# Norm phase of a gated attention/mLSTM layer: the second low part ahead of the modulation sum in two tiles, and wider dummy products

## The chip, the cores and the metric

One core of a Trainium2 chip runs the whole kernel in one launch. The metric is device time in microseconds (us); lower is better. The time before is a median over 3 executions; one further execution was profiled.

The engines are named as in the profile: PE (TensorE, matrix products) with PEld (its weight loads), DVE (VectorE), ACT (ScalarE), POOL (GpSimd) and SP (SyncE, which here issues the DMAs). Each engine works through its own instructions in the order in which the program lists them, and waits only where an operand or a buffer isn't ready.

## The reference, cut to what matters

One layer: a conditioning vector `c` modulates an RMS norm, the result goes through one large projection, then attention and a chunked mLSTM, gates and an output projection. Only the first lines bear on the change:

```
ada = c @ w_ada + b_ada                       # [1, 3*1024]
shift, scale, gate = split(ada, 3)
h = rmsnorm(x, norm_w) * (1 + scale) + shift  # [256, 1024]
... = split(h @ w_in, ...)                    # w_in is [1024, 11272]
```

All is float32, with 256 tokens and a width of 1024.

## The kernel before

**Precision.** A product of two float32 matrices is made of three products of rounded parts: each operand is split into a high part (a cast to the one-pass type fp32r) and a low part (the operand minus its high part), and high·high, high·low and low·high are summed. The high part of a weight tile is a cast on ACT, the low part a subtraction on DVE.

**Norm phase (lines 105 to 311).** The 1024 input features are eight row tiles k = 0..7 of 128. The phase computes the normed and modulated `h` transposed, tile by tile, and at once multiplies each tile with the first 1792 columns of `w_in`, summing over k in four PSUM banks (`pm`, the last one called `pg`). For tile k the DMAs bring `adat[k]`, two halves of [128, 1024] of `w_ada` (s = 1 for scale, s = 0 for shift; four buffers), and `wrow[k]`, the rows of `w_in` in two pieces. The order of all work is written out by hand in the string `P1_STEPS` (lines 42 to 45): one letter for an operation, one digit for a tile or a count. The letters that matter, in their order for a tile k from 1 to 6:

- `b` (L160, ACT): turns the shift sum into a bias column. `i`, `j` (L166, L170, ACT): modulate the tile into `hTh` (high part) and `hf` (full).
- `U` (L183, DVE): low part of `w_in` columns 0 to 511. `G` (L173, DVE): `hTl`, the low part of `h`, from `hf`.
- `x` (L178, ACT): high part of columns 512 to 1023. `L`: SP issues the next two loads.
- `c` of tile k+1 (L152, DVE): the scale sum, a product of `adat[k+1]` with the broadcast `c`, summed along the row. It needs half s = 1 of `adat[k+1]`.
- `z` (L183, DVE): low part of columns 512 to 1023 of tile k. It needs `x`.
- `y` (L178, ACT): high part of columns 1024 to 1791. `a`, `w` of tile k+1 (L156, L178, ACT): scale column from the sum, and the next tile's first high part.
- `k` of tile k+1 (L152, DVE): the shift sum. `v` (L183, DVE): low part of columns 1024 to 1791 of tile k.
- `e` (L194, PE): the tile's 24 products. Bank 0 takes three pairs (with `hTh`·high, `hTh`·low, `hTl`·high), bank 1 three pairs, of which the third uses the low part from `z`, then banks 2 and 3 with high parts, and last the two pairs that use the low part from `v`.

So DVE runs through `U G c z k v` for each tile, and `U` of the next tile follows `v`.

**The beginning.** `keep_clock(n)` (lines 223 to 225) multiplies the identity by itself n times into a PSUM tile that nobody reads. It is called with WARM = 5 ahead of the four products `pc` that spread `c` over the partitions (L233), and again by the step `K5` right behind them. ACT copies `pc` to `cb` (L236), squares the second half of `x` (L239), and makes `diag`, the identity scaled by the reciprocal norm (L242, two halves of tokens, with POOL in between at L213 and L214). Then PE transposes and scales `x` with `diag` as the moving operand (steps D and E, L255), ACT modulates tile 0 out of PSUM (L166), and the products of tile 0 start (step P, L194). DVE computes tile 0's sums at L145, which read `cb`.

**Behind the norm phase** PE goes through the other columns of `w_in` and the three projections (lines 957 to 997), with ACT and DVE splitting each weight tile (L440, L444) a few tiles ahead.

Of the kernel before, what the change touches and what calls it, by code (L numbers as in the profile page):

```python
# [38 lines left out]

P1_STEPS = ("K5 D0 D1 D2 E0 E1 E2 C0 w0 R0 R1 R2 R3 U0 H0 G0 t0 B0 P0 x0 z0 y0 t2 B1 t1 L1 c1 a1 w1 k1 v0 Q0 q0 n0 T3 m0 "
            + "".join(f"b{k} i{k} U{k} j{k} G{k} x{k} " + ("t3 " if k == 2 else "") + f"L2 c{k + 1} z{k} y{k} a{k + 1} "
                      f"w{k + 1} k{k + 1} v{k} e{k} " for k in range(1, 7))
            + "b7 i7 U7 j7 G7 x7 z7 y7 v7 P7 Q7 q7 N7 M7").split()
WARM = 5

KX = 248
NR = 1536 + KX + 8
# [15 lines left out]
def tile_hybrid(ctx: ExitStack, tc: tile.TileContext, x, c, params, params2, w_row, ada_mod, ada_gate,  # L65
                w_in, w_att_proj, w_ml_proj, w_out, out):
    nc = tc.nc
# [15 lines left out]
    ident = consts.tile([128, 128], F32, name="ident")  # L83
# [65 lines left out]
    def modulation_sum(k, s):  # L149
        if s:  # L150
            sums[k] = ph.tile([128, 2], F32, name="sums", bufs=2)
        nc.vector.tensor_tensor_reduce(sq, adat[k][:, s], cb, 1.0, 0.0, OP.mult, OP.add, sums[k][:, s:s + 1])  # L152
# [9 lines left out]
    def modulate(k, parts="ij"):  # L162
        kc = slice(k, k + 1)
        src = xnT[:, k] if k else xps[0][:, 0]
        if "i" in parts:
            nc.scalar.activation(hTh[:, k], src, AF.Identity, scale=Ab[:, kc], bias=Bb[:, kc])  # L166
        if "j" not in parts:
            return
        hf[k] = ph.tile([128, S], F32, name="hf", bufs=2)
        nc.scalar.activation(hf[k], src, AF.Identity, scale=Ab[:, kc], bias=Bb[:, kc])  # L170
# [4 lines left out]
    def split_hi(k, c0, c1, copy=nc.scalar.copy):  # L175
        if k not in wsp:
            wsp[k] = (ph.tile([128, NR], F32R, name="wrh", bufs=3), ph.tile([128, NR], F32R, name="wrl", bufs=3))
        copy(wsp[k][0][:, c0:c1], wrow[k][:, c0:c1])  # L178

    def split_low(k, e, c0, c1):  # L180
        h, l = wsp[k]
        cs = slice(c0, c1)
        e.tensor_tensor(l[:, cs], wrow[k][:, cs], h[:, cs].bitcast(F32), op=OP.subtract)  # L183
# [37 lines left out]
    pw = pp.tile([128, 2, 512], F32, name="warm", tag="pm0")  # L221

    def keep_clock(n):
        for _ in range(n):
            nc.tensor.matmul(pw[:, 0, 0:128], ident, ident, start=True, stop=True)

    keep_clock(WARM)


    pc = [pp.tile([128, 512], F32, name="pc0", tag="pg"), pp.tile([128, D], F32, name="pc1", tag="pm2")]  # L230
    for j in range(4):
        n, q = divmod(j, 2)
        nc.tensor.matmul(pc[n][:, q * 256:(q + 1) * 256], pick[:, j:j + 1].to_broadcast([128, 128]), cparts,  # L233
                         start=q == 0, stop=q == 1, skip_group_check=True)
# [35 lines left out]
    def some(*what):  # L270
        return lambda k: [mm_row(k, ch, (i,)) for ch, i in what]
# [22 lines left out]

    for step in P1_STEPS:
        op, k = step[0], int(step[1])
        if op == "L":
            next_loads(k)
        else:
            dict(C=modulation, H=modulate, R=rel_prep, K=keep_clock, T=x_transposes, t=x_copy, B=open_banks,  # L300
                 D=lambda k: x_transposes(k, (0,)), E=lambda k: x_transposes(k, (1,)),
                 w=lambda k: split_hi(k, 0, 512), x=lambda k: split_hi(k, 512, 1024), y=lambda k: split_hi(k, 1024, NR),
                 U=lambda k: split_low(k, nc.vector, 0, 512), z=lambda k: split_low(k, nc.vector, 512, 1024),
                 v=lambda k: split_low(k, nc.vector, 1024, NR), G=modulate_low,
                 c=lambda k: modulation_sum(k, 1), k=lambda k: modulation_sum(k, 0),
                 a=modulation_scale, b=modulation_shift, i=lambda k: modulate(k, "i"), j=lambda k: modulate(k, "j"),
                 P=lambda k: mm_row(k, 0), Q=lambda k: mm_row(k, 1, (0, 1)), q=lambda k: mm_row(k, 1, (2,)),
                 N=lambda k: mm_row(k, 2), M=lambda k: mm_row(k, 3),
                 n=some((2, 0), (2, 1), (3, 0), (3, 1)), m=some((2, 2), (3, 2)),
                 e=some((0, 0), (0, 1), (0, 2), (1, 0), (1, 1), (1, 2), (2, 0), (2, 1), (3, 0), (3, 1), (2, 2), (3, 2))  # L310
                 )[op](k)
# [187 lines left out]
    f = slice(32, 36)  # L499
# [424 lines left out]
    for g in range(NG):  # L924
# [32 lines left out]
        for kk in range(2):  # L957
            k = 2 * kp + kk
            first, last = k == 0, k == KT - 1
            if ch["name"] == "out":  # L960

                for i in (0, 1):
                    for t, c0 in ((0, 0), (0, 256), (1, 0), (1, 256)):
                        a = (sh_, sl_)[i][:, k, t * 128:(t + 1) * 128]
                        cs = slice(c0, c0 + 256)
                        for w in (wh, wl)[:2 - i]:
                            nc.tensor.matmul(mmt[ci][:, t, cs], a, w[:, kk, cs],  # L967
                                             start=first and i == 0 and c0 == 0 and w is wh,
                                             stop=last and i == 1 and c0 > 0, skip_group_check=True)
            elif ch["kind"] == "tok":  # L970
                for t in range(2):
                    a, b = sh_[:, k, t * 128:(t + 1) * 128], sl_[:, k, t * 128:(t + 1) * 128]
# [14 lines left out]
    for t, c0, n in ((0, 0, 512), (1, 0, 256), (1, 256, 256)):  # L987
        pt = ps.tile([128, n], F32, name="mm", bufs=2)
        for k in range(KT):
            a, b = T["yh"][:, k, t * 128:(t + 1) * 128], T["yl"][:, k, t * 128:(t + 1) * 128]  # L990
# [54 lines left out]
```

## Time and profile before

| | |
|---|---|
| median of 3 runs | 353.72 us (353.4 to 353.92) |
| profiled execution, its own time | 354.01 us |
| its span in the profile | 352.2 us |
| PE busy | 345.3 us (98%) |
| DVE / ACT / POOL busy | 240.7 / 209.9 / 83.0 us |

A row of a timeline gives the start in us from the span's start, the time in us, the engine, the line of the kernel, the operation with output and inputs, how many instructions are merged, and in brackets how long the engine was idle before and what ended that. A row that merges n instructions ends with the end of the last one. Matmuls are pipelined: each is listed with its whole duration though the next starts earlier, so the pace of a row is its time less one duration, over n - 1.

### The profile page before, as it was taken

To read this page: it belongs to the slowest core of one execution; us is meant where nothing else is said; L and a number is where in the kernel's file an instruction comes from. 1 tells how busy PE (TensorE), PEld (TensorE's weight loads), DVE (VectorE), ACT (ScalarE), POOL (GpSimd) and SP (SyncE) were. 2 spreads that over 40 slices of the span, in tenths; PEclk is the share of its full clock that TensorE was granted. 3 is DMA by queue.
4 is the path that set the end of the run, shared out by engine and by line. 5 is a ranking of instruction groups with operands and counts; after the bars stand their busy time and mean duration, and the time that the engine had idled before them with its cause. 6 is when DMAs were issued, how large, how long until landed. Compare 5 with 4: busy or idle time off the path is not lost.

```text
span 352.2 us, 6126 instructions
## 1 busy us (share of the span) xinstructions
PE 345.3 (98%) x2424; PEld 321.0 (91%) x2424; DVE 240.7 (68%) x363; ACT 209.9 (60%) x328; POOL 83.0 (24%) x79
## 2 busy tenths in 40 slices
PE   7999999999999999999999999999999999999996
PEld 6778889888999999999999888888899999999995
DVE  5889988869974428767774474764475775469961
ACT  4867789996885766674654435545646374544510
POOL 4700006582006052555240000000010320452000
PEclk9999999999999999999999999999999999999999
DMA  8999999995680453493664955649219229382011
GB/s 299 418 417 419 412 384 337 237 261 217 220 308 13 139 220 125 147 370 137 239 241 131 378 207 214 265 151 379 66 26 359 95 60 358 123 271 88 2 61 60
DMA packets 25140, 77.98 MB, mean 221 GB/s; under 512 B 2960, under 2 KB 6040, under 8 KB 24600
## 3 DMA queue, kind: packets, MB, share of 16 engines
q1 hardware_dynamic: 24816, 77.03, 61.3%
q10 hardware_dynamic: 296, 0.56, 0.5%
q8 instruction: 19, 0.31, 0.4%
q14 instruction: 9, 0.07, 0.1%
HBM read 76.14 MB, written 1.45 MB: 220 GB/s over the span
## 4 chain that ended last, share of the span: by engine, by line
PE 92%; DMA 7%; DVE 0%; issue 0%; DVEq 0%
PE mm L984 15%; PE mm L981 15%; PE mm L983 15%; PE mm L974 9%; PE mm L975 9%; PE mm L976 9%; PE pm L194 6%; DMA adat<-in_ada_mod_dram 6%; PE mm L967 3%; PE aux L737 1%; PE pg L194 1%; PE mm L996 1%; PE aux L634 1%; PE mm L995 1%; PE mm L994 1%; DMA xt<-in_x_dram 1%
## 5 line engine op out<-in xcount | busy, mean ns | idle before, releaser
L444 DVE TENSOR_TENSOR wl<-raw,wh 128x1024 fp32r<-128x1024 f32 (+1 forms) x92 | 115.8, 1268 | 68.0 <-ACT wh L440 68.0
L440 ACT CAST wh<-raw 128x1024 fp32r<-128x1024 f32 (+1 forms) x100 | 102.2, 1031 | 58.8 <-PE mm L976 29.4
L981 PE MATMUL mm<-hTh,wh 128*128 128x256 f32 x320 | 90.1, 282 | 0.0
L983 PE MATMUL mm<-hTl,wh 128*128 128x256 f32 x320 | 88.7, 277 | 0.0
L984 PE MATMUL mm<-hTh,wl 128*128 128x256 f32 x320 | 88.7, 277 | 0.0
L981 PEld LDWEIGHTS mm<-hTh,wh 128*128 128x128 f32 x320 | 60.2, 188 | 0.1
L983 PEld LDWEIGHTS mm<-hTl,wh 128*128 128x128 f32 x320 | 60.2, 188 | 0.1
L984 PEld LDWEIGHTS mm<-hTh,wl 128*128 128x128 f32 x320 | 60.2, 188 | 0.0
L974 PE MATMUL mm<-wh,hTh 128*128 128x512 f32 (+1 forms) x144 | 55.0, 382 | 0.0
L976 PE MATMUL mm<-wh,hTl 128*128 128x512 f32 (+1 forms) x144 | 54.4, 378 | 0.0
L975 PE MATMUL mm<-wl,hTh 128*128 128x512 f32 (+1 forms) x144 | 54.3, 377 | 0.0
L976 PEld LDWEIGHTS mm<-wh,hTl 128*128 128x128 f32 x144 | 27.0, 188 | 5.1
L974 PEld LDWEIGHTS mm<-wh,hTh 128*128 128x128 f32 x144 | 27.0, 188 | 4.7
L975 PEld LDWEIGHTS mm<-wl,hTh 128*128 128x128 f32 x144 | 27.1, 188 | 4.6
L444 POOL TENSOR_TENSOR wl<-raw,wh 128x1024 fp32r<-128x1024 f32 x8 | 19.5, 2456 | 18.4 <-ACT wh L440 18.4
L774 POOL TENSOR_SCALAR f<-f 128x4 f32<-128x4 f32 x2 | 0.4, 198 | 86.9 <-DVE f L773 86.9
L183 DVE TENSOR_TENSOR wrl<-raw,wrh 128x512 fp32r<-128x512 f32 (+1 forms) x24 | 18.1, 781 | 0.5 <-ACT wrh L178 0.4
L981 PE MATMUL mm<-yah,wh 128*128 128x256 f32 x64 | 18.3, 286 | 0.0
L152 DVE CUSTOM_DVE_ANT_0 sq<-adat,cb 128x1024 f32<-128x1024 f32 x14 | 17.1, 1221 | 1.1 <-DMA adat<-in_ada_mod_dram 1.1
L984 PE MATMUL mm<-yah,wl 128*128 128x256 f32 x64 | 17.7, 277 | 0.0
L983 PE MATMUL mm<-yal,wh 128*128 128x256 f32 x64 | 17.7, 277 | 0.0
L981 PE MATMUL mm<-ymh,wh 128*128 128x256 f32 x64 | 17.7, 276 | 0.0
(218 smaller groups left out, 663.8 us busy)
## 6 DMA issues: line engine op xcount, KB each, us to landing
raw<-in_w_in_dram SPq DMA_DIRECT2D x36, 1024.0 KB, 4.9
adat<-in_ada_mod_dram SPq DMA_DIRECT2D x16, 512.0 KB, 9.3
raw<-in_w_row_dram SPq DMA_DIRECT2D x8, 640.0 KB, 9.4
raw<-in_ada_gate_dram SPq DMA_DIRECT2D x4, 1024.0 KB, 5.6
raw<-in_w_att_proj_dram SPq DMA_DIRECT2D x4, 1024.0 KB, 7.9
raw<-in_w_ml_proj_dram SPq DMA_DIRECT2D x4, 1024.0 KB, 5.5
raw<-in_w_out_dram SPq DMA_DIRECT2D x4, 1024.0 KB, 4.8
raw<-in_w_row_dram SPq DMA_DIRECT2D x8, 256.0 KB, 9.3
```

The source lines that it names most:

```text
L152: nc.vector.tensor_tensor_reduce(sq, adat[k][:, s], cb, 1.0, 0.0, OP.mult, OP.add, sums[k][:, s:s + 1])
L183: e.tensor_tensor(l[:, cs], wrow[k][:, cs], h[:, cs].bitcast(F32), op=OP.subtract)
L194: nc.tensor.matmul(pm[ch][:, t], a[:, k, t * 128:(t + 1) * 128], b[:, cs], start=k == 0 and i == 0 and (ch < 3 or t == 0), stop=k == KT - ...
L440: nc.scalar.copy(h, w)
L444: e.tensor_tensor(l, w, h.bitcast(F32), op=OP.subtract)
L967: nc.tensor.matmul(mmt[ci][:, t, cs], a, w[:, kk, cs], start=first and i == 0 and c0 == 0 and w is wh, stop=last and i == 1 and c0 > 0, sk ...
L974: nc.tensor.matmul(o, a, wh[:, kk], start=first, stop=False)
L975: nc.tensor.matmul(o, a, wl[:, kk], start=False, stop=False)
L976: nc.tensor.matmul(o, b, wh[:, kk], start=False, stop=last)
L981: nc.tensor.matmul(o, wh[:, kk, cs], sh_[:, k], start=first and i % 2 == 0, stop=False, skip_group_check=True)
L983: nc.tensor.matmul(o, wh[:, kk, cs], sl_[:, k], start=False, stop=False, skip_group_check=True)
L984: nc.tensor.matmul(o, wl[:, kk, cs], sh_[:, k], start=False, stop=last and i % 2 == 1, skip_group_check=True)
```

## The change

In tiles 2 and 3 the order of `c` and `z` is swapped, so that DVE makes the second low part of tile k ahead of the scale sum of tile k+1. In the other tiles the order stays. The dummy products at the beginning are 3 instead of 5, in both places, and each has 512 moving columns (the identity four times over) instead of 128.

```diff
-P1_STEPS = ("K5 D0 D1 D2 E0 E1 E2 C0 w0 R0 R1 R2 R3 U0 H0 G0 t0 B0 P0 x0 z0 y0 t2 B1 t1 L1 c1 a1 w1 k1 v0 Q0 q0 n0 T3 m0 "
-            + "".join(f"b{k} i{k} U{k} j{k} G{k} x{k} " + ("t3 " if k == 2 else "") + f"L2 c{k + 1} z{k} y{k} a{k + 1} "
-                      f"w{k + 1} k{k + 1} v{k} e{k} " for k in range(1, 7))
+P1_STEPS = ("K3 D0 D1 D2 E0 E1 E2 C0 w0 R0 R1 R2 R3 U0 H0 G0 t0 B0 P0 x0 z0 y0 t2 B1 t1 L1 c1 a1 w1 k1 v0 Q0 q0 n0 T3 m0 "
+            + "".join(f"b{k} i{k} U{k} j{k} G{k} x{k} " + ("t3 " if k == 2 else "") + f"L2 "
+                      + (f"z{k} c{k + 1} " if k in (2, 3) else f"c{k + 1} z{k} ") + f"y{k} a{k + 1} w{k + 1} k{k + 1} v{k} e{k} " for k in range(1, 7))
             + "b7 i7 U7 j7 G7 x7 z7 y7 v7 P7 Q7 q7 N7 M7").split()
-WARM = 5
+WARM = 3
...
     def keep_clock(n):
         for _ in range(n):
-            nc.tensor.matmul(pw[:, 0, 0:128], ident, ident, start=True, stop=True)
+            nc.tensor.matmul(pw[:, 0].rearrange("p (r n) -> p r n", r=4), ident, ident[:, None, :].to_broadcast([128, 4, 128]),
+                             start=True, stop=True)
```

## The prediction

> **What bounds the kernel now.** I read the page first, for the bound, then PE's own waits, then the timelines of DVE, ACT and PE around the places that the change touches.
>
> ```profile
> span 352.2 us, 6126 instructions
> ...
> PEclk9999999999999999999999999999999999999999
> ...
> PE 92%; DMA 7%; DVE 0%; issue 0%; DVEq 0%
> PE warm L225 <- POOL ident masks.py:199: 1.4, 1, 1.4
> PE xps L255 <- ACT diag L242: 0.8, 1, 0.8
> PE pm L194 <- DVE wrl L183: 0.6, 1, 0.6
> PE pm L194 <- ACT hTh L166: 0.5, 1, 0.5
> ```
>
> The chain that ended last is PE for 92% of the span, and the last four rows are all the waits of PE that the profile lists. The next rows place them: before 25 us. Behind that PE never waits, so whatever the norm phase gains or loses reaches the end one to one, unless a new wait is made. The profiled execution took 354.01 us, 1.8 more than its span; that is 0.3 above the median of the runs, 353.72. I add my sum to both.
>
> ```profile
> 21.31 0.43 DVE L173 TENSOR_TENSOR hTl<-hf,hTh 128x256 fp32r<-128x256 f32 x1
> 22.85 1.22 DVE L152 CUSTOM_DVE_ANT_0 sq<-adat,cb 128x1024 f32<-128x1024 f32 x1 [1.11 <-DMA adat<-in_ada_mod_dram]
> 24.00 0.69 DVE L183 TENSOR_TENSOR wrl<-raw,wrh 128x512 fp32r<-128x512 f32 x1
> 24.60 1.22 DVE L152 CUSTOM_DVE_ANT_0 sq<-adat,cb 128x1024 f32<-128x1024 f32 x1
> 25.75 1.55 DVE L183 TENSOR_TENSOR wrl<-raw,wrh 128x768 fp32r<-128x768 f32 x2
> 27.66 1.22 DVE L152 CUSTOM_DVE_ANT_0 sq<-adat,cb 128x1024 f32<-128x1024 f32 x1
> 29.41 1.22 DVE L152 CUSTOM_DVE_ANT_0 sq<-adat,cb 128x1024 f32<-128x1024 f32 x1
> 30.55 1.56 DVE L183 TENSOR_TENSOR wrl<-raw,wrh 128x768 fp32r<-128x768 f32 x2
> ...
> 24.74 0.73 PE L194 MATMUL pm<-wrl,hTh 128*128 128x512 f32 x2 [0.64 <-DVE wrl L183]
> 25.31 0.63 PE L194 MATMUL pm<-wrh,hTh 128*128 128x512 f32 x2
> 26.76 0.73 PE L194 MATMUL pm<-wrl,hTh 128*128 128x512 f32 x2
> 31.66 0.63 PE L194 MATMUL pm<-wrl,hTh 128*128 128x512 f32 x2
> ```
>
> This is the place that the swap aims at. DVE stands 1.11 us for `adat[3]` with c3 (22.85). z2 (24.00) is queued behind c3 though its input was there, and PE stands 0.64 us for z2. At 26.76 and 31.66 PE takes v2 and v3 (DVE 25.75 and 30.55; each row holds v and the next U, a 512-column subtraction of 0.69 that starts some 0.08 before v ends, so v takes 0.95). So v3 is done at 31.50, only 0.1 us (a semaphore's 0.05 included) ahead of PE. From here on PE has almost nothing in hand on DVE: the sums repeat every 29.41 − 24.60 = 4.81 us, and PE's tiles every 4.8 (31.66 − 26.76 = 4.90, of which 0.1 is a refill after a wait). A stall that goes is worth no more than what v3 allows.
>
> **The swap, with nothing else changed.** No instruction is added. ACT's and SP's orders stay (`x`, `y`, `a`, `w`, the loads), and no queue but DVE's is changed. What is late next is seen in two more groups.
>
> ```profile
> 12.51 1.22 DVE L152 CUSTOM_DVE_ANT_0 sq<-adat,cb 128x1024 f32<-128x1024 f32 x1
> 13.77 1.23 DVE L152 CUSTOM_DVE_ANT_0 sq<-adat,cb 128x1024 f32<-128x1024 f32 x1
> ...
> 21.18 0.61 ACT L178 CAST wrh<-raw 128x512 fp32r<-128x512 f32 x1
> 25.87 0.29 ACT L160 ACTIVATE Bb<-sums,prm 128x1 f32<-128x1 f32 x1 [0.81 <-DVE sums L152]
> 26.70 0.59 ACT L170 ACTIVATE hf<-xnT,Bb,Ab 128x256 f32<-128x256 f32 x1
> 27.19 1.35 ACT L178 CAST wrh<-raw 128x512 fp32r<-128x512 f32 x2
> ```
>
> The first two rows are c1 and k1 back to back: 1.26 from start to start, where c3 to z2 is 24.00 − 22.85 = 1.15. Two sums in a row cost 0.11 more. In the new order z2 follows x2 (ACT 21.18 to 21.79) in the wait, c3 stays at 22.85, and k3 starts at 24.11 instead of 24.60. Then b3, i3, j3, x3 on ACT come 0.49 earlier (x3 from 26.70 to 27.31) and G3 too. But in tile 3 z now stands ahead of c4 and there is no DMA wait to fill: G3 is over at 27.2, z3 waits for x3 until 27.36, c4 starts at 27.97 (0.31 later than before) and k4 at 29.23. What is left is 29.41 − 29.23 = 0.18 us, and v3 carries it to PE. Bounds: were `adat[3]` there as soon as z2 is done, c3 could start at 22.43 and DVE would be some 0.5 us ahead at k4; were v3 no bound at all, PE would gain its 0.64, the refill behind it (24.74 to 25.31 is 0.57, where later pairs take 0.46) and 0.06 at 26.76, 0.8 in all.
>
> **The dummy products.** They delay PE, and here lies the larger term.
>
> ```profile
> 1.35 2.50 PE L225 MATMUL warm<-ident 128*128 128x128 f32 x10 [1.35 <-POOL ident masks.py:199]
> 1.94 1.27 PE L225 MATMUL warm<-ident 128*128 128x128 f32 x5
> 3.94 1.23 PE L233 MATMUL pc<-cparts,pick 128*128 128x256 f32 x4
> 5.38 0.84 PE L225 MATMUL warm<-ident 128*128 128x128 f32 x6
> 7.24 2.94 PE L255 MATMUL xps<-diag,xt 128*128 128x128 f32 x24 [0.79 <-ACT diag L242]
> 10.68 0.74 PE L194 MATMUL pm<-wrh,hTh 128*128 128x512 f32 x2 [0.50 <-ACT hTh L166]
> 74.08 0.43 PE aux L596 x2
> ...
> 4.78 1.07 ACT L236 COPY cb<-pc 128x512 f32<-128x512 f32 x2 [1.78 <-PE pc L233]
> 5.74 1.07 ACT L239 ACTIVATE xnT<-xt 128x1024 f32<-128x1024 f32 x1
> 7.89 0.40 ACT L242 ACTIVATE diag<-ident,rsx 128x128 f32<-128x128 f32 x1 [0.70 <-POOL rsx L214]
> 10.06 0.56 ACT L166 ACTIVATE hTh<-xps,Bb,Ab 128x256 fp32r<-128x256 f32 x1 [0.43 <-DVE Bb L145]
> ```
>
> Five products are ten records, so one float32 product is two. Their pace is (1.27 − 0.42)/4 = 0.21 us in the first row of five and (0.84 − 0.28)/5 = 0.11 from 5.38 on: the clock doubles there, 4.03 us after the first product. The page's PEclk shows nines in all slices, so it doesn't tell of this. Does a record grow with its columns? 256 columns take 0.43/2 = 0.215 (L596) at the fast clock against 0.11 for 128, so it does; 512 columns are 0.85 slow and 0.43 fast. No row has a 512-column float32 product: the low end would be one pass, half of that.
>
> By the Trainium skill, page "TensorE: Matmul & The Clock Gate", section "What's actually happening", the clock is freed after one busy window of about 3.4 us that runs free of the kernel's start. The 4.03 us here agree with it; what it would make of other executions stands with the third rival.
>
> First batch, six records: it starts at 1.35, the first has 0.16 of fill (1.94 less 1.35 is 0.59 for two paces of 0.21), so the fifth starts at 4.92. If the clock rises at 5.38 as before, the rest of it takes 0.20, the sixth 0.43, and `pc` starts at 6.0 instead of 3.94. `pc` runs at 0.11 instead of 0.21 apiece, so the copies to `cb`, 0.84 behind the start of `pc` before, come 0.35 behind: 6.35 instead of 4.78. ACT has no slack up to `diag` (copies, square and first `diag` follow each other), so the second `diag` is at 9.5 instead of 7.89. PE meanwhile does its second batch: `pc` is over at 6.45, six records of 0.43 end at 9.03, so the transposes start there, instead of 7.24. Their 24 records at 0.11 end at 11.7; tile 0's own part needs the first 16 of them, 10.8 plus a drain of 0.2. hTh0 so starts at 11.0 instead of 10.06, and the first products at 11.7 instead of 10.68. Before, PE had 0.79 and 0.50 us of waiting here that would have hidden 1.3 us; the two batches add more than that. `cb` at 7.5 makes L145 only 0.3 later, which this covers.
>
> **The sum.** All of tiles 0 and 1 is a chain through ACT and DVE without slack, so both reach tile 2 late by 11.0 − 10.06, 0.95 us. There the DVE wait takes part of it: x2 ends at 22.74, z2 starts behind it, c3 0.60 later at 23.35 (0.50 late, `adat[3]` is there), and k3 1.26 later at 24.61, level with before. PE, late by about 1 and with no stall at 24.1, takes v2 at 26.87, 0.1 late. In tile 3, x3 is as before (27.20 to 27.80), so z3 can't start before 27.85, c4 starts at 28.46 (0.80 late), k4 at 29.72, v3 at 30.87: 0.32 late. PE waits 0.2 for v3 at 31.66, plus a refill of 0.1. Tiles 4 to 6 repeat this at 4.81, so nothing is won back. Net +0.32 us: the swap in tile 2 pays for the dummies, the swap in tile 3 costs 0.3. That gives 354.33 us for the profiled execution and 354.04 by the median; I take 354.1. A measurement of this kernel can tell about 0.2%, 0.7 us, from no change.
>
> **The rivals.**
> - *The dummies cost nothing*, because a record is one pass or the clock rises with them much earlier. If a record were one pass, six would end by about 4.1 and the start would be as before. Then the swap alone counts: −0.18 to −0.5, 353.2 to 353.5. For it: PE waits at 7.24 and 10.68. Against it: the 256-column row. 0.2.
> - *The stall goes whole*, v3 giving way because its tile ran early: −0.8, 352.9. It needs the first rival and `adat` halves earlier by over a microsecond as well. 0.1.
> - *The clock rises later than at 5.38*, and the long dummies run at half speed. Before, this would be hidden up to about 8 us, as the transposes wait for `diag` and hTh0 for DVE's shift column, so the runs' narrow spread says nothing against it. Now every microsecond of it costs half a microsecond of PE's start: at 6.5 +0.9, at 8.2 +1.7, and from 6.2 on it is over 0.7, slower: 354.6 to 355.4. 0.25.
> - The forecast, with the clock between 4.4 and 6.2: −0.1 to +0.7. 0.45.
>
> By the page of the Trainium skill named with the clock, a free-running window would put the rise anywhere between 3.4 and 6.8 us after the first product, an estimate of −0.0 to +1.7 us; one trace can't show how it is spread.
>
> **How the numbers follow.** 353.2 is the low end (the first rival's), 355.0 the high end (a clock at some 7.2 us); less than 2 in 10 lies outside. Faster by over 0.2%: 0.1 of the second rival and a few hundredths for unknown terms of the first, 0.13. Slower: the late clock, 0.25, and a little for the forecast's upper edge, 0.28. Same: 0.59.
>
> **What would show it.** In the profile after: `warm` records with a pace of 0.85 and 0.43; `pc` near 6.0, hTh0 near 11.0; no wait of PE for z2; z2 in front of c3 and c3 without a DMA wait; c4 late behind z3; a PE wait of 0.1 to 0.2 at v3; k4 0.3 later than 29.41. It is wrong if hTh0 starts near 10.1, if the clock rises far from 5.4, or if PE waits somewhere behind 35 us.

## The result and the profile after

The changed kernel takes 355.62 us (median of 5 runs, 355.35 to 356.02) beside 353.72 for the kernel before on the same chip (5 runs, 353.4 to 354.05): a ratio of 1.0055 with a 95% interval of 1.0041 to 1.0069. It is slower by 1.9 us, where 0.3 was forecast, and lies above the range. The profiled execution took 355.64 us with a span of 353.9; the one of before took 354.01 with 352.2. From line 226 on, the changed kernel's lines are one higher.

The page, its span and the shares of the chain of waits by engine, and then the view of waits, PE's own rows in full:

```profile
span 353.9 us, 6110 instructions
...
PE 97%; POOL 1%; ACT 1%; issue 0%; DVE 0%; POOLq 0%
```

```profile
PE warm L225 <- POOL ident masks.py:199: 1.4, 1, 1.4
PE xps L256 <- ACT diag L243: 1.1, 1, 1.1
```

PE waits less than before: the 0.6 us for z2 and the 0.5 for `hTh` have gone. Yet the span is 1.7 us longer. So the time is lost where PE is busy or held up early, and the timeline of PE says where:

```profile
1.35 4.75 PE L225 MATMUL warm<-ident 128*128 128x512 f32 x6 [1.35 <-POOL ident masks.py:199]
5.54 1.03 PE L234 MATMUL pc<-cparts,pick 128*128 128x256 f32 x4
6.40 2.74 PE L225 MATMUL warm<-ident 128*128 128x512 f32 x6
8.98 1.50 PE L256 MATMUL xps<-diag,xt 128*128 128x128 f32 x12
11.57 1.60 PE L256 MATMUL xps<-diag,xt 128*128 128x128 f32 x12 [1.09 <-ACT diag L243]
12.94 0.72 PE L194 MATMUL pm<-wrh,hTh 128*128 128x512 f32 x2
...
33.21 0.73 PE L194 MATMUL pm<-wrl,hTh 128*128 128x512 f32 x2
```

The 24 transposes, one run of instructions before, fall into two halves. The second half waits for the second `diag`, and the first products start at 12.94 instead of 10.68. The last row is the product that takes v3: 33.21 instead of 31.66. ACT's rows show what `diag` waited for:

```profile
6.37 1.07 ACT L237 COPY cb<-pc 128x512 f32<-128x512 f32 x2 [3.38 <-PE pc L234]
8.38 0.40 ACT L243 ACTIVATE diag<-ident,rsx 128x128 f32<-128x128 f32 x1
11.12 0.40 ACT L243 ACTIVATE diag<-ident,rsx 128x128 f32<-128x128 f32 x1 [2.34 <-POOL rsx L214]
```

The two halves of `diag` are 2.74 us apart, because ACT waited 2.34 us for POOL. POOL's two instructions there and DVE's at the same time, first after, then before:

```profile
8.58 0.83 POOL L213 TENSOR_SCALAR rsx<-ssx 128x1 f32<-128x1 f32 x1 [1.99 <-ACT xnT L240]
9.49 1.59 POOL L214 TENSOR_TENSOR rsx<-rsx,mhalf 128x1 f32<-128x1 f32 x1
```

```profile
7.98 1.34 DVE L145 CUSTOM_DVE_ANT_0 sq<-adat,cb,b 128x1024 f32<-128x1024 f32 x1 [2.01 <-DMA adat<-in_ada_mod_dram]
9.37 1.29 DVE L145 CUSTOM_DVE_ANT_0 sq<-adat,cb,prm 128x1024 f32<-128x1024 f32 x1
```

```profile
6.98 0.22 POOL L213 TENSOR_SCALAR rsx<-ssx 128x1 f32<-128x1 f32 x1 [0.31 <-ACT xnT L239]
7.29 0.57 POOL L214 TENSOR_TENSOR rsx<-rsx,mhalf 128x1 f32<-128x1 f32 x1
7.81 0.87 POOL L279 COPY rvec<-prm 8x16 f32<-8x16 f32 x1
```

```profile
7.28 1.34 DVE L145 CUSTOM_DVE_ANT_0 sq<-adat,cb,b 128x1024 f32<-128x1024 f32 x1 [1.29 <-ACT diag L242]
```

The same two instructions on 128 numbers take 0.83 and 1.59 us instead of 0.22 and 0.57. After, L213 starts inside DVE's first sum (7.98 to 9.32) and ends 0.09 behind that sum's end; L214 starts inside the second sum (9.37 to 10.66) and ends 0.42 behind its end. Before, L213 was over by 7.20 and L214 started with the sum (7.29 and 7.28; at that distance the rows don't say which was first), and neither was held. But the row behind them was: a copy of 8 by 16 numbers, begun inside the sum, takes 0.87 us there. The Trainium skill, page "SBUF — State Buffer", section "SBUF: two separate sides", says that a DVE instruction with two SBUF inputs and a GpSimd instruction that reads SBUF exclude each other for a whole instruction, and that whichever starts first goes first. L145 has two such inputs, `adat` and `cb`. These rows agree with it where POOL comes second. No run here shows the other direction: where a sum begins inside L214 (e6, below), it isn't any longer.

Of the swap, DVE's rows in tiles 2 and 3:

```profile
24.07 0.69 DVE L183 TENSOR_TENSOR wrl<-raw,wrh 128x512 fp32r<-128x512 f32 x1
24.68 1.22 DVE L152 CUSTOM_DVE_ANT_0 sq<-adat,cb 128x1024 f32<-128x1024 f32 x1
25.94 1.22 DVE L152 CUSTOM_DVE_ANT_0 sq<-adat,cb 128x1024 f32<-128x1024 f32 x1
...
29.18 0.69 DVE L183 TENSOR_TENSOR wrl<-raw,wrh 128x512 fp32r<-128x512 f32 x1
29.78 1.22 DVE L152 CUSTOM_DVE_ANT_0 sq<-adat,cb 128x1024 f32<-128x1024 f32 x1
31.05 1.22 DVE L152 CUSTOM_DVE_ANT_0 sq<-adat,cb 128x1024 f32<-128x1024 f32 x1
```

These are z2, c3, k3 and z3, c4, k4. c3 has no DMA wait any more, as forecast, but k3 is at 25.94 (24.60 before) and k4 at 31.05 (29.41 before).

### The profile page after: what moved, and what is told of

Its sections match the earlier page's. It is cut to its first block, busy times and chain, and to the rows that moved or that the text cites. A ratio compares the mean times of both kernels' runs of the same rounds, so it can differ in the third digit from the quotient of the medians.

```text
span 353.9 us, 6110 instructions
## 1 busy us (share of the span) xinstructions
PE 347.9 (98%) x2416; PEld 320.1 (90%) x2416; DVE 241.4 (68%) x363; ACT 210.1 (59%) x328; POOL 82.0 (23%) x79
## 4 chain that ended last, share of the span: by engine, by line
PE 97%; POOL 1%; ACT 1%; issue 0%; DVE 0%; POOLq 0%
PE mm L982 15%; PE mm L984 14%; PE mm L985 14%; PE pm L194 10%; PE mm L975 9%; PE mm L977 9%; PE mm L976 9%; PE mm L968 3%; PE pg L194 2%; PE aux L738 1%; PE warm L225 1%; PE aux L635 1%; PE mm L996 1%; PE mm L997 1%; PE mm L995 1%; PE aux L485 1%
## 5 line engine op out<-in xcount | busy, mean ns | idle before, releaser
L183 DVE TENSOR_TENSOR wrl<-raw,wrh 128x512 fp32r<-128x512 f32 (+1 forms) x24 | 18.1, 778 | 2.1 <-ACT wrh L178 1.8
L984 PE MATMUL mm<-yml,wh 128*128 128x256 f32 x64 | 17.7, 276 | 0.0
```

The source lines that it names most:

```text
L984: nc.tensor.matmul(o, wh[:, kk, cs], sl_[:, k], start=False, stop=False, skip_group_check=True)
```

## The experiments

Two theories stood at the start. **POOL held up:** the wide dummies push the second root on POOL under DVE's sums, which delays `diag`; the swap matters little. **Dummies on PE, or the swap:** the longer PE work itself, or z ahead of c, makes the time. Each diff is against the changed kernel unless it says otherwise. The kernel before was run again on the same chips; its medians there were 353.6 to 353.72.

**e1, the swap alone.** Against the kernel before, only the order string is changed.

```diff
-f"L2 c{k + 1} z{k} y{k} ..."
+f"L2 " + (f"z{k} c{k + 1} " if k in (2, 3) else f"c{k + 1} z{k} ") + f"y{k} ..."
```

> Theory (the wide dummies cost all of it: they push the second reciprocal root, L213 and L214 on POOL, under DVE's two sums of tile 0, and it stands until each has ended): with the narrow dummies of before the start is as before (first products of tile 0 at 10.7, L213 and L214 about 0.2 and 0.6 us each time), z2 is no wait of PE any more, and the time is 0.2 to 0.5 us below before: 353.2 to 353.5. Rival (the new order itself costs, by z3 ahead of c4 and two sums in a row): 354.0 or more.

Measured: 354.08 us, ratio 1.001 (1.0001 to 1.0019). The forecast of a gain missed: no time is won, some 0.4 us is lost, and the interval only just excludes no change.

**e2, the dummies alone.** Against the kernel before, the wide products, WARM = 3 and K3; the order of before.

> Theory: tile 0's first products start at 12.9 as in the changed kernel (2.26 us late). DVE's wait for the fourth pair of halves and PE's wait for z2 take some of this back, and nothing is lost at z3: about 1.3 us above before, 355.0, so 0.3 to 0.6 below the changed kernel. Rival (the order is what costs): within 0.3 us of before, 353.7.

Measured: 355.28 us, ratio 1.0041 (1.0029 to 1.0054). Most of the loss is the dummies'. Its L213 and L214 took 0.38 and 1.59 us.

**e3, POOL's root away from the sums.** The square of the second half of `x` goes from ACT to DVE, so that POOL has its input earlier.

```diff
-nc.scalar.activation(xnT[:, 4:8].rearrange("p k s -> p (k s)"), xt[:, 1], AF.Square, scale=1.0 / 32, accum_out=ssx[:, 1:2])
+nc.vector.tensor_tensor_reduce(sq, xt[:, 1], xt[:, 1], 1.0 / D, 0.0, OP.mult, OP.add, ssx[:, 1:2])
```

> The squares of the second half of x are summed on DVE behind those of the first half, so that POOL has the second root done by about 8.0, before or just as DVE's sums of tile 0 start; the wide dummies stay. Theory: L213 and L214 take about 0.2 and 0.6 both times, the second diag follows the first (about 8.0), tile 0's hTh starts near 11.0 and its products at 11.7 as the prediction had it; about 0.3 us above before: 353.9 to 354.3. Rival (the wide products, or the late time itself, slow POOL): L214 still over 1 us, time as the changed kernel, 355.4 to 355.9.

Measured: 354.6 us, ratio 1.0019 (1.0009 to 1.0028), above what was expected; but about 1.0 us of the 1.9 comes back with all six wide dummies in place. POOL's rows, then PE's:

```profile
5.64 1.31 POOL L213 TENSOR_SCALAR rsx<-ssx 128x1 f32<-128x1 f32 x1 [3.46 <-DVE ssx L238]
...
7.71 0.22 POOL L213 TENSOR_SCALAR rsx<-ssx 128x1 f32<-128x1 f32 x1
8.02 0.57 POOL L214 TENSOR_TENSOR rsx<-rsx,mhalf 128x1 f32<-128x1 f32 x1
```

```profile
1.36 5.35 PE L225 MATMUL warm<-ident 128*128 128x512 f32 x6 [1.36 <-POOL ident masks.py:199]
9.58 2.84 PE L256 MATMUL xps<-diag,xt 128*128 128x128 f32 x24
```

The second root takes 0.22 and 0.57 again, and the transposes are one run. Now the first L213 is held (1.31), by the DVE square that was put at 5.64 beside it: the same effect in another place, on a root whose half of `diag` (7.93) is still in time for the transposes at 9.58. What is left here is PE's own dummies, whose first batch took 5.35 us in this execution, 0.6 more than in the changed kernel's.

**e4, only the first batch wide,** the second `K5` narrow as before; swaps kept.

```diff
-P1_STEPS = ("K3 D0 ...
+P1_STEPS = ("K5 D0 ...
...
-            nc.tensor.matmul(pw[:, 0].rearrange("p (r n) -> p r n", r=4), ident, ident[:, None, :].to_broadcast([128, 4, 128]),
-                             start=True, stop=True)
+            if n == 3:
+                nc.tensor.matmul(pw[:, 0].rearrange("p (r n) -> p r n", r=4), ident,
+                                 ident[:, None, :].to_broadcast([128, 4, 128]), start=True, stop=True)
+            else:
+                nc.tensor.matmul(pw[:, 0, 0:128], ident, ident, start=True, stop=True)
```

> The first batch wide (3 of 512 columns), the second as before (5 of 128). Theory: the first batch alone makes the copies to cb and all of ACT late (6.4 instead of 4.8), so the second root meets DVE's sums as in the changed kernel: second diag at 11.1, tile 0's products at 12.9, time within 0.3 us of the changed kernel, 355.3 to 355.9. Rival (the second batch holds up the transposes, and that costs): the products of tile 0 at or below 11.7, time 353.5 to 354.3.

Measured: 355.68 us, ratio 1.0055 (1.0042 to 1.0067), the changed kernel's own. POOL's rows (in e4, e6 and e10 the lines behind `keep_clock` are four higher than before the change):

```profile
8.95 0.43 POOL L213 TENSOR_SCALAR rsx<-ssx 128x1 f32<-128x1 f32 x1 [2.40 <-ACT xnT L243]
9.47 1.59 POOL L214 TENSOR_TENSOR rsx<-rsx,mhalf 128x1 f32<-128x1 f32 x1
```

Of the dummies, the first batch alone does the harm. It is ahead of `pc`, and so ahead of `cb`, ACT's square and POOL's root; the second batch is only ahead of the transposes.

**e5, the swap in tile 2 only,** narrow dummies: e1 with `k == 2` in place of `k in (2, 3)`.

> The swap in tile 2 alone, narrow dummies. Theory (in tile 3 there is no DMA wait to fill: z3 waits for x3, and two sums in a row cost 0.1, so that c4 comes 0.3 late): k4 some 0.3 us earlier than with both swaps against the same c3, v3 as well, and the time 0.3 to 0.4 below the run with both swaps: 353.3 to 353.7. Rival (the swaps don't matter to the time, only how late the fourth pair of halves lands): the same as with both, 354.0 to 354.2.

Measured: 353.76 us, ratio 1.0001 (0.9993 to 1.001). Inconclusive by the time, which is at the kernel before's and just above the range expected; its profile has a place in the table below.

**e6, only the second batch wide,** swaps kept: the `keep_clock` of e4 with WARM = 5 and `K3`.

> The second batch wide, the first as before, both swaps. Theory (the first batch costs all of it): pc at 3.9, second root ahead of DVE's sums (0.2 and 0.6 us), second diag at 7.9; the second batch ends at 7.8 to 8.5 by when the clock rises, and tile 0's products start at 10.7 to 11.2; the time is that of the swaps alone up to 0.4 more: 353.9 to 354.5. Rival (either batch is enough to cost the time): 355 or more.

Measured: 353.63 us, ratio 0.9999 (0.9989 to 1.001), below what was expected. PE's rows:

```profile
4.51 3.20 PE L226 MATMUL warm<-ident 128*128 128x512 f32 x6
7.55 2.84 PE L259 MATMUL xps<-diag,xt 128*128 128x128 f32 x24
10.66 0.74 PE L194 MATMUL pm<-wrh,hTh 128*128 128x512 f32 x2 [0.27 <-ACT hTh L166]
```

Three wide products behind `pc` cost nothing. The transposes start at 7.55, right behind them, 0.3 later than in the profile of before, and PE still waits 0.27 us for `hTh` (0.50 before). In this execution DVE's first sum began inside L214, POOL and then DVE:

```profile
7.17 0.57 POOL L214 TENSOR_TENSOR rsx<-rsx,mhalf 128x1 f32<-128x1 f32 x1
```

```profile
7.26 1.35 DVE L145 CUSTOM_DVE_ANT_0 sq<-adat,cb,b 128x1024 f32<-128x1024 f32 x1 [1.28 <-DMA adat<-in_ada_mod_dram]
```

Neither is longer than elsewhere (0.57, and 1.34 to 1.35 us).

**e10, the same with the order of before,** so against the kernel before only `K5` becomes a wide `K3`.

> Only the second batch wide, narrow first batch, the order of before. Theory: the second batch is hidden behind ACT and DVE as it was with the swaps, and the swaps' 0.3 each is not paid: 353.2 to 353.7, at or a little below before. Rival (the swaps gain 0.4 and the wide second batch costs 0.4): 353.9 to 354.2.

Measured: 353.59 us, ratio 0.9995 (0.9984 to 1.0006). That is no change that can be told; no version here beats the kernel before by more than the noise.

**e7 and e11, DVE's sums held back.** A small DVE copy that reads the second root is put ahead of tile 0's sums, so DVE has no two-input instruction running while POOL works. In e7 it writes a new tile, in e11 an existing one.

```diff
+held = consts.tile([128, 1], F32, name="held")   # e7
+nc.vector.tensor_copy(held, rsx[:, 1:2])         # e7
+nc.vector.tensor_copy(qns, rsx[:, 1:2])          # e11
```

> The changed kernel, with one small copy on DVE of the second root ahead of tile 0's sums, so that DVE does nothing while POOL works on that root, which is as late as in the changed kernel. Theory (POOL stands under DVE's sums): L213 and L214 take 0.2 and 0.6 us again, the second diag is at 9.5, L145 starts at about 9.5 and tile 0's hTh at about 12.2, now after DVE's sums; the time as the changed kernel within 0.3. Rival (POOL is slow because of the wide products on PE, or so late): L213 and L214 0.4 to 0.8 and 1.6 us as before.

> As the run with the sums held back, but the small copy goes to a tile that is there already, so that no address moves. Theory: L213 and L214 take 0.2 and 0.6 us; L145 starts at about 9.6 instead of 8.0 and now sets tile 0's hTh (12.3 to 12.7); 355.5 to 356.2, and PE's products of 256 columns keep the 0.113 us from one to the next that they have before. Rival (the copy or the order itself cost the 7 us, not the moved addresses): 360 or more.

Measured: e7 362.78 us (one run), e11 356.34, ratio 1.0074 (1.006 to 1.0088), a little above what was expected. The views of e11, POOL and then DVE:

```profile
8.85 0.22 POOL L213 TENSOR_SCALAR rsx<-ssx 128x1 f32<-128x1 f32 x1 [2.45 <-ACT xnT L240]
9.15 0.57 POOL L214 TENSOR_TENSOR rsx<-rsx,mhalf 128x1 f32<-128x1 f32 x1
```

```profile
10.11 1.34 DVE L145 CUSTOM_DVE_ANT_0 sq<-adat,cb,b 128x1024 f32<-128x1024 f32 x1
11.50 1.28 DVE L145 CUSTOM_DVE_ANT_0 sq<-adat,cb,prm 128x1024 f32<-128x1024 f32 x1
```

POOL's input comes as late as in the changed kernel (8.85 beside 8.58), the dummies are the same, and DVE is idle: 0.22 and 0.57. So it is DVE's sums that stretch POOL's work. The kernel is no faster, since the sums now start 2.13 us later (10.11 beside 7.98) and the bias column waits for them. e7's POOL rows are 0.22 and 0.57 as well; its further 6.4 us are another thing (last section).

**e8, the kernel before, profiled once more.**

> The kernel before once more, for a second look at what differs from one execution to the next: when the first and the fourth pair of halves land, when the clock rises, and how long DVE stands at c3. If the DVE wait at c3 comes with every execution: 0.5 to 1.2 us and PE's wait for z2 0.2 to 0.7. If it is of one execution only: under 0.3, and then the swap has nothing to fill and can only cost. Time 353.2 to 354.3.

Measured: 353.57 us, span 351.8. DVE's rows and PE's:

```profile
22.10 0.42 DVE L173 TENSOR_TENSOR hTl<-hf,hTh 128x256 fp32r<-128x256 f32 x1
22.44 1.22 DVE L152 CUSTOM_DVE_ANT_0 sq<-adat,cb 128x1024 f32<-128x1024 f32 x1
23.58 0.69 DVE L183 TENSOR_TENSOR wrl<-raw,wrh 128x512 fp32r<-128x512 f32 x1
24.19 1.22 DVE L152 CUSTOM_DVE_ANT_0 sq<-adat,cb 128x1024 f32<-128x1024 f32 x1
...
28.99 1.22 DVE L152 CUSTOM_DVE_ANT_0 sq<-adat,cb 128x1024 f32<-128x1024 f32 x1
```

```profile
4.51 2.34 PE L225 MATMUL warm<-ident 128*128 128x128 f32 x10
...
11.48 0.74 PE L194 MATMUL pm<-wrh,hTh 128*128 128x512 f32 x2 [1.60 <-ACT hTh L166]
```

c3 starts at 22.44, 0.34 behind G2, with no DMA wait; z2 follows at 23.58, and PE doesn't wait for it. So the wait of 1.11 us that the swap was to fill is in only one of two profiled executions of this kernel. In part that is the later start: this execution started its products 0.8 us later (11.48 beside 10.68) and so asks for `adat[3]` at 22.44, where the other, by the same 0.34 behind G2, would have started c3 at 21.65. It was still 0.4 us faster.

**e9, the swap in tiles 2 to 6,** narrow dummies: e1 with `k in (2, 3, 4, 5, 6)`.

> The swap in tiles 2 to 6, narrow dummies. Theory (where no DMA wait is there to fill, z ahead of c puts DVE behind x of the same tile and sets two sums side by side, which makes a tile's round through DVE and ACT 5.1 us instead of 4.81, and PE waits for v in each): 0.3 per further tile, so 0.8 to 1.0 above the run with tiles 2 and 3: 354.8 to 355.1, k4 to k5 to k6 5.1 apart. Rival (the order is free, and the runs with it were slower by chance of the landings): 353.8 to 354.3, k sums 4.8 apart.

Measured: 354.96 us, ratio 1.0039 (1.0026 to 1.0053). DVE's rows, G, z, c and k of one tile and the next k:

```profile
26.45 0.43 DVE L173 TENSOR_TENSOR hTl<-hf,hTh 128x256 fp32r<-128x256 f32 x1
26.96 0.69 DVE L183 TENSOR_TENSOR wrl<-raw,wrh 128x512 fp32r<-128x512 f32 x1
27.56 1.22 DVE L152 CUSTOM_DVE_ANT_0 sq<-adat,cb 128x1024 f32<-128x1024 f32 x1
28.83 1.22 DVE L152 CUSTOM_DVE_ANT_0 sq<-adat,cb 128x1024 f32<-128x1024 f32 x1
...
33.93 1.22 DVE L152 CUSTOM_DVE_ANT_0 sq<-adat,cb 128x1024 f32<-128x1024 f32 x1
```

These k are 5.10 us apart where the kernel before has 4.81. The 0.29 is seen in the rows: z starts 0.51 behind G (it waits for `x` on ACT), where c starts 0.34 behind G in e8, and c to k takes 1.27 where c to z takes 1.14 (23.58 − 22.44). 0.17 + 0.13 is 0.30.

**Side by side,** without e7 and e9, whose later parts differ as well. The columns are starts in us from the timelines: DVE's second sum of tile 0 (the later of the two L145), PE's first product of tile 0, and DVE's k3 and k4.

| kernel | dummies | swap in | second L145 | first product | k3 | k4 | span |
|---|---|---|---|---|---|---|---|
| before, the prediction's profile | narrow | none | 8.67 | 10.68 | 24.60 | 29.41 | 352.2 |
| before, again (e8) | narrow | none | 9.47 | 11.48 | 24.19 | 28.99 | 351.8 |
| e10 | second wide | none | 9.28 | 11.29 | 24.01 | 29.12 | 351.9 |
| e1 | narrow | 2, 3 | 9.25 | 11.26 | 24.26 | 29.36 | 352.2 |
| e5 | narrow | 2 | 9.48 | 11.49 | 24.48 | 29.29 | 352.6 |
| e6 | second wide | 2, 3 | 8.65 | 10.66 | 23.65 | 28.81 | 351.7 |
| e2 | both wide | none | 8.98 | 12.55 | 25.27 | 30.07 | 352.9 |
| e4 | first wide | 2, 3 | 9.35 | 12.91 | 25.91 | 31.01 | 353.8 |
| changed | both wide | 2, 3 | 9.37 | 12.94 | 25.94 | 31.05 | 353.9 |
| e3 | both wide | 2, 3 | 9.47 | 12.18 | 25.19 | 30.29 | 352.9 |
| e11 | both wide | 2, 3 | 11.50 | 13.51 | 26.56 | 31.66 | 354.5 |

Three distances repeat. From the second L145 to the first product it is 2.01 us wherever POOL's root is short and done in time; it is 3.56 or 3.57 in the three kernels whose first batch is wide and whose root lies under the sums, and 2.71 in e3, where the transposes start late but nothing is held. From the first product to k3 it is 12.71 or 12.72 without a swap in tile 2 and 12.99 to 13.05 with it (13.92 with the DMA wait at c3 in the prediction's profile). From k3 to k4 it is 4.80 or 4.81 without a swap in tile 3 and 5.10 to 5.16 with it (5.11 in e10, where c4 waits 0.21 us for its DMA). And span less k4 is 322.8 or 322.9 in all but two rows (e5 323.3, e3 322.6). So the change is 3.57 − 2.01 = 1.56 us for the first batch and 0.28 + 0.30 for the two swaps, 2.14 in all. From e8 to the changed kernel, whose sums start 0.10 earlier, that makes 2.04; k4 moves by 2.06 and the span by 2.1. The medians differ by 1.9. They show less of the swaps than these starts do: 0.34 us between e2 and the changed kernel, 0.45 for e1, 0.03 for e6. Executions in which a swap has a DMA wait to fill would explain that, but which of the runs had one isn't known.

## Why the prediction was wrong

**Right, by its steps.** PE is the bound, and what the beginning loses reaches the end. Its dummies come out at the row it took them from: the second batch has a pace of (2.74 − 0.59)/5 = 0.43 us, as forecast (0.59 is the time of one record of it), the copies to `cb` start at 6.37 (6.35), the transposes at 8.98 (9.03). `pc` is listed at 5.54 rather than 6.0, though the sixth dummy record starts only at 5.51. The waits for z2 and of c3 for its DMA are gone. The working of tiles 2 and 3 holds too, counted from the first product: 11.7 forecast gave k3 at 24.61 and k4 at 29.72, 12.9 and 18.0 later, and 12.94 gave 25.94 and 31.05, 13.0 and 18.1 later.

**The step that failed** is "so the second `diag` is at 9.5 instead of 7.89". It is at 11.12. The step added ACT's delay and took POOL's two instructions between square and `diag` at their old durations. But the dummies moved the root from 6.98 to 8.58 while DVE's first sum moved from 7.28 to 7.98 and no further: POOL was moved into DVE's two sums. (In the changed kernel the sum waited for the DMA of `adat[0]`. The row of before names `diag` instead, but the sum can't need it: in the changed kernel it starts ahead of both halves of `diag`.) The prediction asked only whether L145 would be late ("only 0.3 later, which this covers"), not what it runs beside. Nor does an engine wait only where an operand or a buffer isn't ready, as is said at the start: L213 and L214 had started, and were stretched all the same. The row that warned of it was in the profile of before: 0.87 us for a copy of 8 by 16 numbers at 7.81, under the first sum. In e8 the same copy ahead of the sums takes 0.19. With 1.24 us more at the first product (12.94 less 11.7), 0.32 becomes 1.56; the two profiled executions differ by 1.63.

**The second error** is the reference. The prediction carried the 0.3 us by which the profiled execution was above the median over to the changed kernel. That 0.3 belongs to the wait of c3 and PE's stall behind it, which e8 doesn't have: from the first product to k4 it is 18.73 us in the prediction's profile and 17.51 in e8, and the first product 0.80 us earlier made up for only part of that. What takes the wait away takes the 0.3 away as well, so against the median the change costs that much more, 1.9. The same error made the swap look like a gain of 0.18: in an execution without the wait there is nothing to fill, and z ahead of c costs 0.28 to 0.30 a tile. The prediction had worked out this cost for tile 3 (0.31) and offset it by a wait in tile 2 that e8 doesn't have.

**The rivals.** That the dummies cost nothing is wrong of the first batch (e4) and right of the second (e6, e10). That the stall goes whole and is gained is not borne out: in e1 it is gone, and the time is 0.45 above. A later clock gave 354.6 to 355.4, near the result, but it wasn't the cause: in the changed kernel the fifth and sixth record start at 4.93 and 5.51, 0.58 apart where the slow pace is 0.85 and the fast one 0.43, so the clock rose between them, inside the forecast's 4.4 to 6.2. The instant does differ between executions: e8's ten narrow records from 4.51 on have a pace of (2.34 − 0.42)/9 = 0.21 us, still the slow one, up to 6.85, where the profile of before had the fast one from 5.38 on. The Trainium skill, page "TensorE: Matmul & The Clock Gate", section "What's actually happening", has the window run free of the kernel's start; these two agree with that. In e8 PE waits for `hTh` for 1.60 us behind it, and the late clock costs nothing. With a wide first batch a later rise does lengthen it: in e3 the fifth and sixth record start 0.85 apart (4.93 and 5.78), and the batch is 0.6 us longer.

**What stays open.** What sets the landing of the `adat` halves, which makes tile 0's first sum start anywhere from 7.26 to 8.09 in kernels that hold nothing back, and the wait for `adat[3]` appear in one execution and not in another, wasn't found. For the second the traces hold a candidate. A view of the DMA queues from 20 to 22 us of the prediction's profile (packets, MB, share of 16 engines) has one packet among the data that isn't data:

```profile
q8 instruction: 1, 0.02, 3.0%
```

3.0% of 16 engines over 2 us is 0.96 us on one of them. It starts between 20.6 and 20.9 us, shortly before c3 gets `adat[3]` at 22.85. In e8 it starts between 21.3 and 21.6; in e10 it is behind 22.9, and there c4 waits 0.21 us for `adat[4]`. That it holds back a load is argued from these times, not shown; e9 has it between 20.7 and 21.0, and its c3, asked for only at 22.46, doesn't wait. As the landings differ, e6 against e1 stays unsettled: with the same swaps its median is 0.45 us lower, and its profile starts its sums 0.6 us earlier, for which its wide second batch gives no reason that was tried.

## What to carry to other kernels

Before an edit moves work in time, look at what the other engines do at the place to which it is moved, not only at whether the operands are there: a tiny instruction on the critical path can be stretched by a large neighbour. A stall that one profile shows is worth a second profile before an edit is built on it; if it is not there, the edit's own cost is all that is left. And an offset between a profiled execution and the median belongs to something; find out to what, before adding it to both sides.

## What the runs showed of the hardware that was not expected

- POOL instructions on 128 numbers took 0.83 and 1.59 us under DVE's two-input sums and 0.22 and 0.57 without them, in the changed kernel and e11; in e3 a DVE square beside it made 1.31 of 0.24.
- e7 and e11 differ only in whether the copy's target is a new tile of 4 bytes a partition, and e7 is 6.4 us longer. The groups by line show it in PE's products, here the first of three large groups, e11 and then e7 (busy us, mean ns of one):

```profile
L983 PE MATMUL mm<-hTh,wh 128*128 128x256 f32 x320 | 90.1, 282 | 0.0
```

```profile
L984 PE MATMUL mm<-hTh,wh 128*128 128x256 f32 x320 | 91.1, 285 | 0.0
```

  3 ns a product over some 2400 products is 7 us; PE's busy time is 354.7 us beside 348.2. That the tile shifts what is allocated behind it is argued, not shown; no run moved the tiles by another amount.
